# The z projection of a hybrid SSD encoder by groups of 512 columns in four PSUM banks, and a decay tile per direction

## The chip, the core and the metric

The kernel runs on one NeuronCore of a Trainium2 chip, on float32 data. The metric is the device time of one execution in microseconds (us). The engines are TensorE (PE: matmuls and transposes into PSUM banks), VectorE (DVE), ScalarE (ACT), GpSimd (POOL) and SyncE (SP, which issues the loads of weights).

## The reference

Two encoder layers over 512 tokens of width 1024. Each has a token-mixing sub-layer with one wide input projection, a pooling mixer and a bidirectional SSD mixer, and then a gated MLP with a depthwise convolution. What the change touches is the input projection's z part, the SSD mixer and its gated norm:

```python
proj = x @ w_in
u_pool, z, xbc, dt_raw, gate_logits = jnp.split(proj, list(IN_SPLITS), axis=-1)
xbc = jax.nn.silu(dwconv_centred(xbc, ssd_conv_w, ssd_conv_b))
xs, bm, cm = jnp.split(xbc, [SSD_INNER, SSD_INNER + gn], axis=-1)
y = bidirectional_ssd(xh, dt_raw, a_log, dt_bias, bm, cm, d_skip)
# per direction and head, by chunks of 128 tokens:
decay = jnp.exp(jnp.where(lower, a_cum[l] - a_cum[s], -jnp.inf))
y_diag = (C B^T * decay) x          # and a state carried from chunk to chunk
# gated norm, per group of 512 columns
v = y * jax.nn.silu(z)
v = v * lax.rsqrt(jnp.mean(v * v, axis=-1, keepdims=True) + RMS_EPS)
ssd_out = (v * g) @ w_ssd_proj
```

z and the SSD's inner width have 2048 columns: four groups of 512 columns, eight units of 256 columns (four heads of 64 each).

## The kernel before, in words

Every projection is made of three float32r matmuls per product (`mm3`, L297): each operand is cut into a high part and a remainder (`wh`, `wl` for weights, `xth`, `xtl` for x, transposed). `WeightStream` (L39) loads weight blocks of 1 MB through SP's queue into two buffers, and `_split` (L77) makes each half of a block into `wh` by a cast on ACT (L90) and `wl` by a subtraction on DVE (L91), three pairs of buffers. `get(ahead)` hands out the next pair and starts the splits `ahead` places on. The order of the blocks is written by `weight_plan` (L145).

Two PSUM pools have four banks each of 128x512 float32 (L252 to L260): `bank_a` for the projections, `bank_b` for small products and transposes. A bank goes to its next user when all readers of the last one are done.

PE's order is the order of the program text (`manual_schedule`, L280); the other engines get theirs from the scheduler, and each engine takes its instructions in its own fixed order. `Background` (L112) holds jobs, Python generators that emit a small piece of PE work and yield how many ticks their successor's data need. A tick, called between the matmuls of a projection, emits at most one piece, of the first job in the list that is ready.

For each layer and each group g of four (L1019): the columns B and C of the group (`bc`, two tiles of 128 features by 512 tokens), then unit 2g and unit 2g+1. `unit(u)` (L715) makes two x tiles (`xp`: 24 matmuls each, the weights stationary, 512 tokens moving), and gives each to `conv_silu` (L567): `conv` (L386) reads the bank by one ACT pass (L389) and four DVE taps (L395), and a Silu on ACT follows (L570). Then it makes the unit's z, token-major: for each of four chunks of 128 tokens, x's tile is stationary and 256 weight columns move, 8 x 3 matmuls per chunk, two chunks in one bank; a Silu (L736) takes each bank to `zs`.

Jobs run behind that: `bc_job` (transpose `btp`, scores `scp`), `x_job` (transpose `xt` to `xtok`), `unit_job` (L800: the weighted x `xw` on POOL, states `stp`, L835, their outputs `yop`, L862, then `zs` times `y`, L881, and per group `norm` with the squares `sq`, L891, and the transposes `ytp`), `heads_job` (L746) with `decay(h)` (L754) and the products `ydp` (L786). `decay` fetches the cumulative sums of both directions by one DMA on ACT's queue into a tile m of [128, 2, 512], masks each half on POOL (L761), takes eight exponentials of 128x128 on ACT (L768) and adds the halves on DVE (L769). Behind group 0 the dt job is finished, and behind group g > 0 the output projection `spp` of group g-1 runs (L922).

Of the kernel before, what the change touches and what calls it, by code (L numbers as in the profile page):

```python
# [9 lines left out]
F32 = mybir.dt.float32  # L10
# [7 lines left out]
P = 128  # L18
# [93 lines left out]
class Background:  # L112
    """Small pieces of TensorE work, put between the matmuls of the projections: one piece at
    most per tick; a piece says after how many ticks its successor's data can be there."""
# [5 lines left out]
    def spawn(self, gen, delay=0):  # L120
        job = Job(gen, self.now + delay)
        self.jobs.append(job)
        return job
# [21 lines left out]
def weight_plan(l, w_in, pool_w, w_ssd_proj, w_out, w_up, w_down):  # L145
# [37 lines left out]
    def unit(u):  # L183
        return pair(w_in, OFF_X + 256 * u) + ktiles(w_in, 0, KD, OFF_Z + 256 * u, 256)
# [37 lines left out]
def tile_hybrid_pool_ssd_convffn_encoder(  # L222
# [120 lines left out]
    def feature_tiles(name, n):  # L343
        """n column tiles [128 features, 512 tokens] of the next weights times x."""
# [12 lines left out]
    def first_tiles(name, n, fresh=False):  # L357
        """The same, by halves of the tokens, with what is left of x's transposes in between."""
# [27 lines left out]
    def conv(dst, ps, taps, bias):  # L386
        """Centred depthwise convolution along the tokens; taps are per-feature columns."""
# [12 lines left out]
    def rsqrt(pool, v, name):  # L400
        """v ** -0.5 of positive columns: a guess from the bits, then Newton's iteration."""
# [12 lines left out]
    def token_projection(l, name, src_h, src_l, kn, xcs, lnp, gt, bt, finish, final=False):  # L414
        """x <- LayerNorm(ALPHA * x + src @ w), token-major, by chunks of 128 tokens."""
# [9 lines left out]
        def root(c, mv):  # L425
            """(variance + EPS) ** -0.5, with a step of Newton's iteration."""
# [10 lines left out]
        def pieces(half, c):  # L437
            """The columns of a half that are summed and finished together."""
# [96 lines left out]
    for l in range(NL):  # L535
        # per-feature parameters as columns
# [46 lines left out]
        def make_bc(g, tiles):  # L583
# [4 lines left out]
            return bg.spawn(bc_job(g, bt, ct), 10)  # L588
# [126 lines left out]
        def unit(u):  # L715
# [3 lines left out]
            for i in range(2):  # L719
                (xps,) = feature_tiles(f"xp{nm}_{i}_", 1)  # L720
                cv = conv_silu(xps, 2 * u + i, f"xc{nm}_{i}")
                xjobs.append(bg.spawn(x_job(u, i, cv, xtok), 11))
            zs = sp.tile([P, NCH, 256], F32, tag="zs", name=f"zs{nm}", bufs=3)
            wz = [ws.get() for _ in range(2)]
            for cc in range(2):
                ps = bank_a(f"zp{nm}_{cc}")
                for ci in range(2):
                    c = 2 * cc + ci
                    s = slice(c * P, (c + 1) * P)
                    for k in range(KD):  # L730
                        wh, wl = wz[k // 4]
                        mm3(ps[:, ci * 256 : (ci + 1) * 256], xts["h"][:, k, s], xts["l"][:, k, s],
                            wh[:, k % 4, :], wl[:, k % 4, :], k == 0, k == KD - 1)
                        if k % 4 == 3:
                            bg.tick()
                nc.scalar.activation(  # L736
                    zs[:, 2 * cc : 2 * cc + 2, :],
                    ps.rearrange("p (c n) -> p c n", c=2), AF.Silu,
                )

            return bg.spawn(unit_job(u, xtok, zs, xjobs), 1)
# [4 lines left out]
        def heads_job():  # L746
            """The masked decay matrices of the heads, both directions, and the products with
            them within the chunks of 128 tokens."""
# [51 lines left out]
        def unit_job(u, xtok, zs, xjobs):  # L800
# [78 lines left out]
            while heads_done[0] < 4 * u + 4:  # L879
                yield 0  # L880
# [298 lines left out]
```

## Time and profile before

| what | value |
|---|---|
| median of 3 runs | 1991.07 us (1989.05 to 1992.81) |
| span of the profiled execution, first to last instruction | 1990.3 us |
| mean granted TensorE clock | 0.994 |
| PE busy | 1954.0 us, 98% |
| DVE busy | 1179.1 us, 59% |
| ACT busy | 947.9 us, 48% |
| POOL busy | 430.9 us, 22% |

The profiled execution has no time of its own beside its span; the span lies 0.8 us under the median of the runs. PE's rows overlap, because a matmul's row lasts until its modelled end; what a matmul costs in a stream is the step from one start to the next. The SSD stretch of layer 0, which the change rewrites, reaches from about 33 to 420 us, that of layer 1 from about 1020 to 1390 us.

### The profile page before, as it was taken

To read this page: it belongs to the slowest core of one execution; us is meant where nothing else is said; L and a number is where in the kernel's file an instruction comes from. 1 tells how busy PE (TensorE), PEld (TensorE's weight loads), DVE (VectorE), ACT (ScalarE), POOL (GpSimd) and SP (SyncE) were. 2 spreads that over 40 slices of the span, in tenths; PEclk is the share of its full clock that TensorE was granted. 3 is DMA by queue.
4 is the path that set the end of the run, shared out by engine and by line. 5 is a ranking of instruction groups with operands and counts; after the bars stand their busy time and mean duration, and the time that the engine had idled before them with its cause. 6 is when DMAs were issued, how large, how long until landed. Compare 5 with 4: busy or idle time off the path is not lost.

```text
span 1990.3 us, 27038 instructions
## 1 busy us (share of the span) xinstructions
PE 1954.0 (98%) x10614; PEld 1643.9 (83%) x10614; DVE 1179.1 (59%) x1796; ACT 947.9 (48%) x1629; POOL 430.9 (22%) x456
## 2 busy tenths in 40 slices
PE   8999999999999999999999999999999999999998
PEld 7878798988888888888888888989888888888886
DVE  5568576775556655543475685667656566555334
ACT  4767666644332544431257776656443334444321
POOL 1344424241111111110003344252411111111000
PEclk9999999999999999999999999999999999999999
DMA  5443424233241323232325434443333413322321
GB/s 159 127 116 116 127 92 141 85 112 114 79 162 51 106 94 110 94 128 92 97 93 154 115 112 118 116 120 104 90 111 91 169 43 106 106 85 92 129 89 72
DMA packets 172160, 214.87 MB, mean 108 GB/s; under 512 B 6752, under 2 KB 127748, under 8 KB 172032
## 3 DMA queue, kind: packets, MB, share of 16 engines
q1 hardware_dynamic: 151376, 170.14, 26.9%
q10 hardware_dynamic: 17712, 34.08, 6.5%
q0 software_dynamic: 2944, 8.91, 1.4%
q8 instruction: 84, 1.38, 0.3%
q14 instruction: 44, 0.36, 0.1%
HBM read 208.66 MB, written 4.46 MB: 107 GB/s over the span
## 4 chain that ended last, share of the span: by engine, by line
PE 86%; issue 7%; ACT 2%; DVE 2%; POOL 1%; DMA 1%; SPq 0%; ACTq 0%; POOLq 0%; DVEq 0%
PE fg L300 7%; PE fg L299 7%; PE fg L298 7%; PE dp L298 4%; PE dp L299 4%; PE dp L300 4%; PE spp L298 3%; PE spp L299 3%; PE spp L300 3%; PE zp L298 3%; PE zp L299 3%; PE zp L300 3%; PE xp L298 2%; PE xp L299 2%; PE xp L300 2%
## 5 line engine op out<-in xcount | busy, mean ns | idle before, releaser
L91 DVE TENSOR_TENSOR wl<-wraw,wh 128x1024 fp32r<-128x1024 f32 (+1 forms) x318 | 395.8, 1246 | 394.9 <-ACT wh L90 393.6
L90 ACT CAST wh<-wraw 128x1024 fp32r<-128x1024 f32 (+1 forms) x318 | 328.4, 1035 | 434.2 <-PE dp L300 121.9
L300 PE MATMUL fg<-xthm,wl 128*128 128x512 f32 x640 | 249.0, 389 | 0.0
L298 PE MATMUL fg<-xthm,wh 128*128 128x512 f32 x640 | 249.0, 389 | 0.0
L299 PE MATMUL fg<-xtlm,wh 128*128 128x512 f32 x640 | 249.0, 389 | 0.0
L768 ACT ACTIVATE m<-m,nac 128x128 f32<-128x128 f32 x512 | 158.5, 389 | 53.1 <-POOL m L761 52.8
L1122 POOL TENSOR_TENSOR cvv<-cvv,cg 128x512 f32<-128x512 f32 x44 | 56.6, 1286 | 412.8 <-DVE cvv L395 382.0
L299 PEld LDWEIGHTS fg<-xtlm,wh 128*128 128x128 f32 x640 | 120.2, 188 | 25.0
L298 PEld LDWEIGHTS fg<-xthm,wh 128*128 128x128 f32 x640 | 120.2, 188 | 24.9
L300 PEld LDWEIGHTS fg<-xthm,wl 128*128 128x128 f32 x640 | 120.2, 188 | 24.8
L298 PE MATMUL dp<-wh,ah 128*128 128x512 f32 (+1 forms) x352 | 136.6, 388 | 0.0
L300 PE MATMUL dp<-wh,al 128*128 128x512 f32 (+1 forms) x352 | 136.4, 387 | 0.0
L299 PE MATMUL dp<-wl,ah 128*128 128x512 f32 (+1 forms) x352 | 136.4, 387 | 0.0
L761 POOL TENSOR_SCALAR_AFFINE_SELECT m<-m 128x512 f32<-128x512 f32 x128 | 95.0, 767 | 179.6 <-DMA m<-acd 136.8
L298 PE MATMUL spp<-yth,wh 128*128 128x512 f32 x256 | 110.3, 431 | 0.5 <-ACT yth L916 0.5
L876 POOL TENSOR_TENSOR y<-y,yo 128x256 f32<-128x256 f32 x96 | 85.9, 904 | 103.0 <-DVE yo L868 100.2
L299 PE MATMUL spp<-ytl,wh 128*128 128x512 f32 x256 | 101.2, 395 | 0.7 <-DVE ytl L917 0.7
L300 PE MATMUL spp<-yth,wl 128*128 128x512 f32 x256 | 101.1, 395 | 0.0
L395 DVE SCALAR_TENSOR_TENSOR xc<-xp,pcwc,xc 128x510 f32<-128x510 f32 (+1 forms) x128 | 95.2, 745 | 7.7 <-ACT xc L389 6.1
L1125 ACT CAST ah<-cvv 128x512 fp32r<-128x512 f32 x44 | 27.3, 621 | 147.2 <-POOL cvv L1122 147.2
L512 POOL TENSOR_TENSOR x<-x,lnb 128x512 f32<-128x512 f32 x15 | 20.2, 1345 | 325.7 <-DVE x L508 316.1
L769 DVE TENSOR_TENSOR m<-m 128x512 f32<-128x512 f32 x64 | 45.8, 716 | 64.2 <-ACT m L768 54.9
(347 smaller groups left out, 4779.1 us busy)
## 6 DMA issues: line engine op xcount, KB each, us to landing
wraw<-in_w_in_dram SPq DMA_DIRECT2D x56, 1024.0 KB, 5.5
wraw<-in_w_up_dram SPq DMA_DIRECT2D x44, 1024.0 KB, 5.1
m<-acd ACTq DMA_DIRECT2D x64, 512.0 KB, 4.9
wraw<-in_w_down_dram SPq DMA_DIRECT2D x20, 1024.0 KB, 5.1
wraw<-in_w_ssd_proj_dram SPq DMA_DIRECT2D x16, 1024.0 KB, 5.1
wraw<-in_w_in_dram SPq DMA_DIRECT2D x16, 512.0 KB, 5.5
wraw<-in_w_out_dram SPq DMA_DIRECT2D x8, 1024.0 KB, 5.3
xi<-in_x_dram SPq DMA_DIRECT2D x4, 512.0 KB, 6.9
```

The source lines that it names most:

```text
L90: self.nc.scalar.copy(hv, src)
L91: self.nc.vector.tensor_tensor(lv, src, hv, op=ALU.subtract)
L298: nc.tensor.matmul(ps, lhsT=ah, rhs=bh, start=first, stop=False)
L299: nc.tensor.matmul(ps, lhsT=ah, rhs=bl, start=False, stop=False)
L300: nc.tensor.matmul(ps, lhsT=al, rhs=bh, start=False, stop=last)
L395: nc.vector.scalar_tensor_tensor(dst[:, o0:o1], ps[:, o0 + s : o1 + s], tap, dst[:, o0:o1], op0=ALU.mult, op1=ALU.add,)
L761: nc.gpsimd.affine_select(out=mv, in_=mv, pattern=[[0, NCH], [1 - 2 * d, P]], compare_op=ALU.is_ge, fill=NEG, base=0, channel_multiplier=2 ...
L768: nc.scalar.activation(mc, mc, AF.Exp, bias=nac[:, c, col : col + 1])
L769: nc.vector.tensor_tensor(m[:, 0], m[:, 0], m[:, 1], op=ALU.add)
L876: nc.gpsimd.tensor_tensor(y[:, c, :], y[:, c, :], yo[:, d, :], op=ALU.add)
L1122: nc.gpsimd.tensor_tensor(cv, cv, cg, op=ALU.mult)
L1125: nc.scalar.copy(h, cv)
```

## The change

`unit(u)` is taken apart. `x_unit(u)` makes the two x tiles and spawns the unit's job at once. `z_group(g)` runs once per group, between the two x units: z for 512 columns, four chunks of tokens in four banks. Its weight blocks are [512 rows of w_in, 512 columns], cut into four pairs of two 128-row tiles (two blocks and four pairs per group, as before). The first two pairs go through all four banks in turn, four products of 128 rows in each bank; with the last two pairs each chunk is finished and goes through its Silu. There are 16 ticks per group, as before. `bc_job` and `x_job` now go to the head of the list of jobs, and `bc_job` waits 7 ticks for 10. `decay` has a tile per direction, `m` (three buffers) and `mb` (two), each with a DMA of its own. `unit_job` waits for `zs_of[u]`. The pooling mixer sums in place, with its edge products taken first.

```diff
-    def unit(u):
-        return pair(w_in, OFF_X + 256 * u) + ktiles(w_in, 0, KD, OFF_Z + 256 * u, 256)
+    def xunit(u):
+        return pair(w_in, OFF_X + 256 * u)
+
+    def zgroup(g):
+        return [s for k in (0, 4) for s in ktiles(w_in, k, k + 4, OFF_Z + 512 * g, 512)]
...
-        seq += bc(g) + unit(2 * g) + unit(2 * g + 1)
+        seq += bc(g) + xunit(2 * g) + zgroup(g) + xunit(2 * g + 1)
...
-    def spawn(self, gen, delay=0):
+    def spawn(self, gen, delay=0, first=False):
         job = Job(gen, self.now + delay)
-        self.jobs.append(job)
+        self.jobs.insert(0 if first else len(self.jobs), job)
...
-            return bg.spawn(bc_job(g, bt, ct), 10)
+            return bg.spawn(bc_job(g, bt, ct), 7, True)
...
-                xjobs.append(bg.spawn(x_job(u, i, cv, xtok), 11))
-            zs = sp.tile([P, NCH, 256], F32, tag="zs", name=f"zs{nm}", bufs=3)
-            wz = [ws.get() for _ in range(2)]
-            for cc in range(2):
-                ps = bank_a(f"zp{nm}_{cc}")
...
+                xjobs.append(bg.spawn(x_job(u, i, cv, xtok), 11, True))
+            return bg.spawn(unit_job(u, xtok, xjobs), 1)
+
+        def z_group(g):
+
+            zg = sp.tile([P, NCH, 512], F32, tag="zs", name=f"zs{l}_{g}", bufs=2)
+            banks = [bank_a(f"zp{l}_{g}_{c}") for c in range(NCH)]
+
+            def product(c, k, wh, wl, kk):
+                s = slice(c * P, (c + 1) * P)
+                mm3(banks[c], xts["h"][:, k, s], xts["l"][:, k, s],
+                    wh[:, kk, :], wl[:, kk, :], k == 0, k == KD - 1)
+
+            for b in range(2):
+                wh, wl = ws.get()
+                for kk in range(2):
+                    for c in range(NCH):
+                        product(c, 2 * b + kk, wh, wl, kk)
+                        if c % 2:
                             bg.tick()
+            got = [ws.get(1) for _ in range(2)]
+            for c in range(NCH):
+                for b in range(2):
+                    wh, wl = got[b]
+                    for kk in range(2):
+                        product(c, 4 + 2 * b + kk, wh, wl, kk)
+                    bg.tick()
+                nc.scalar.activation(zg[:, c, :], banks[c], AF.Silu)
+            for i in range(2):
+                zs_of[2 * g + i] = zg[:, :, i * 256 : (i + 1) * 256]
...
-                m = sp.tile([P, 2, T], F32, tag="m", name=f"m{l}_{h}", bufs=3)
-                nc.scalar.dma_start(
-                    m, acd[l].rearrange("(d h) t -> d h t", d=2)[:, h, :].partition_broadcast(P)
-                )
-                for d in range(2):
-                    mv = m[:, d].rearrange("p (c t) -> p c t", c=NCH)
+                m = sp.tile([P, T], F32, tag="m", name=f"m{l}_{h}", bufs=3)
+                mb = sp.tile([P, T], F32, tag="mb", name=f"mb{l}_{h}", bufs=2)
+                for d, t in enumerate((m, mb)):
+                    col = d * 32 + h
+                    nc.scalar.dma_start(t, acd[l][col : col + 1, :].partition_broadcast(P))
...
-            while heads_done[0] < 4 * u + 4:
+            while heads_done[0] < 4 * u + 4 or u not in zs_of:
                 yield 0
+            zs = zs_of[u]
...
-            ujobs.append(unit(2 * g))
-            ujobs.append(unit(2 * g + 1))
+            ujobs.append(x_unit(2 * g))
+            z_group(g)
+            ujobs.append(x_unit(2 * g + 1))
```

The instructions move with it. PE's list has 9014 rows before and 8246 after, and ACT's list 85 table loads before and 125 after. In the rows below a line number is that of the file they come from, `xp_4_1` is the second x tile of unit 4, `zp_4_0` the first z bank of unit 4 (before), `zp_2_0` to `zp_2_3` the four z banks of group 2, whose units are 4 and 5 (after).

PE in layer 0 where z follows the x tiles of unit 4, before:

```order
L298 MATMUL xp_4_1_0_2620<-xthi,wh_2466 128x512
L299 MATMUL xp_4_1_0_2620<-xtli,wh_2466 128x512
L300 MATMUL xp_4_1_0_2620<-xthi,wl_2467 128x512
L298 MATMUL zp_4_0_2663<-wh_2536,xthi 128x256 [waits DVE_49,Activation_49]
L299 MATMUL zp_4_0_2663<-wl_2537,xthi 128x256 [waits DVE_49]
L300 MATMUL zp_4_0_2663<-wh_2536,xtli 128x256
```

PE at the same place after the change; `scp_2` is the score product of `bc_job`:

```order
L600 MATMUL scp_2_2452<-ct_2_2346,bt_2_2339 128x128 [waits DVE_49,Activation_49]
L600 MATMUL scp_2_2452<-ct_2_2346,bt_2_2339 128x128 x3
L301 MATMUL zp_2_0_2467<-wh_2356,xthi 128x512
L302 MATMUL zp_2_0_2467<-wl_2357,xthi 128x512
L303 MATMUL zp_2_0_2467<-wh_2356,xtli 128x512
L301 MATMUL zp_2_1_2468<-wh_2356,xthi 128x512
L302 MATMUL zp_2_1_2468<-wl_2357,xthi 128x512
L303 MATMUL zp_2_1_2468<-wh_2356,xtli 128x512
L301 MATMUL zp_2_2_2469<-wh_2356,xthi 128x512 [waits DVE_49]
L302 MATMUL zp_2_2_2469<-wl_2357,xthi 128x512
L303 MATMUL zp_2_2_2469<-wh_2356,xtli 128x512
L301 MATMUL zp_2_3_2470<-wh_2356,xthi 128x512 [waits DVE_49,Activation_49]
```

Before, z's first bank follows the x tile directly, and its rows wait for the weights. After, four banks are opened within twelve matmuls behind a `scp` piece, and the third and the fourth bank wait for DVE, the fourth for ACT as well.

DVE around the taps of that second x tile, before:

```order
L395 SCALAR_TENSOR_TENSOR xc_4_1_2645<-xp_4_1_0_2620,pcwc,xc_4_1_2645 128x510 [waits Activation_49]
L779 TENSOR_TENSOR m_16_2303<-m_16_2303,sct_2_2712 128x512 [waits Activation_49]
L395 SCALAR_TENSOR_TENSOR xc_4_1_2645<-xp_4_1_0_2620,pcwc,xc_4_1_2645 128x511 [waits DVE_49]
L779 TENSOR_TENSOR m_17_2363<-m_17_2363,sct_2_2712 128x512
L395 SCALAR_TENSOR_TENSOR xc_4_1_2645<-xp_4_1_0_2620,pcwc,xc_4_1_2645 128x511 [waits DVE_49]
L917 SCALAR_TENSOR_TENSOR ytl_1_2549<-ytp_1_0_2740,pcbc,yth_1_2548 128x512 [waits Activation_49]
L395 SCALAR_TENSOR_TENSOR xc_4_1_2645<-xp_4_1_0_2620,pcwc,xc_4_1_2645 128x510 [waits DVE_49]
L779 TENSOR_TENSOR m_18_2417<-m_18_2417,sct_2_2712 128x512
```

DVE around the same taps after the change (`m` decay tiles, `sct` the scores, `rs` the sum of the squares of the norm):

```order
L398 SCALAR_TENSOR_TENSOR xc_4_0_2399<-xp_4_0_0_2360,pcwc,xc_4_0_2399 128x510 [waits DVE_49]
L91 TENSOR_TENSOR wl_2474<-wraw_2471,wh_2473 128x1024 [waits DMAHW0_49,PE_49,Activation_49]
L793 TENSOR_TENSOR m_16_2187<-m_16_2187,sct_2_2457 128x512 [waits Activation_49]
L793 TENSOR_TENSOR m_17_2249<-m_17_2249,sct_2_2457 128x512
L398 SCALAR_TENSOR_TENSOR xc_4_1_2459<-xp_4_1_0_2410,pcwc,xc_4_1_2459 128x510 [waits PE_49,Activation_49]
L793 TENSOR_TENSOR m_18_2308<-m_18_2308,sct_2_2457 128x512
L398 SCALAR_TENSOR_TENSOR xc_4_1_2459<-xp_4_1_0_2410,pcwc,xc_4_1_2459 128x511 [waits DVE_49] x2
L910 TENSOR_TENSOR rs_1_2503<-ss_1_2486 128x4 [waits Activation_49]
L398 SCALAR_TENSOR_TENSOR xc_4_1_2459<-xp_4_1_0_2410,pcwc,xc_4_1_2459 128x510 [waits DVE_49]
```

The four taps stand in both behind and between products with the scores; now a weight remainder and two products stand ahead of the first tap, and the norm's sum ahead of the last.

ACT ahead of its pass over that x tile, after the change:

```order
L590 ACT_TABLE_LOAD [waits DVE_49]
L590 ACTIVATE ct_2_2346<-ct_2_2346 128x512 [waits Activation_49]
L782 ACT_TABLE_LOAD [waits DMAHW3_49]
L782 ACTIVATE mb_20_2728<-mb_20_2728,nac_672 128x128 [waits Pool_49]
L595 COPY btok_2_2439<-btp_2_2440 128x512 [waits PE_49]
L90 CAST wh_2473<-wraw_2471 128x1024 [waits DMAHW0_49,PE_49]
L906 ACTIVATE sq_1_0_0_2487,ss_1_2486<-zs_1_1191 128x256 [waits Pool_49]
L573 ACT_TABLE_LOAD [waits DVE_49]
L573 ACTIVATE xc_4_0_2399<-xc_4_0_2399 128x512 [waits Activation_49]
L602 COPY sct_2_2457<-scp_2_2452 128x512 [waits PE_49]
L392 ACTIVATE xc_4_1_2459<-xp_4_1_0_2410,pcbc,pcwc 128x512
```

And before:

```order
L389 ACTIVATE xc_4_0_2609<-xp_4_0_0_2540,pcbc,pcwc 128x512 [waits PE_49]
L90 CAST wh_2655<-wraw_2653 128x1024 [waits DMAHW6_49,PE_49]
L570 ACTIVATE xc_4_0_2609<-xc_4_0_2609 128x512 [waits DVE_49,Activation_49]
L592 COPY btok_2_2688<-btp_2_2689 128x512 [waits PE_49]
L389 ACTIVATE xc_4_1_2645<-xp_4_1_0_2620,pcbc,pcwc 128x512 [waits PE_49]
L599 COPY sct_2_2712<-scp_2_2707 128x512
```

The pass over the second x tile (`xc_4_1<-xp_4_1`) now has the three table loads, the square and the score copy ahead of it; before, the copy of the scores came behind it.

## Rows read from the trace of the kernel before

**Rows 1.** the page's span and busy time: us, share, instructions.
```profile
span 1990.3 us, 27038 instructions
...
PE 1954.0 (98%) x10614; PEld 1643.9 (83%) x10614; DVE 1179.1 (59%) x1796; ACT 947.9 (48%) x1629; POOL 430.9 (22%) x456
```

**Rows 2.** waits of PE: us in total, times, longest.
```profile
PE stp L835 <- POOL xw L818: 6.5, 4, 2.1
```

**Rows 3.** timeline of PE, z of unit 7, 24 starts: start, us.
```profile
384.31 0.28 PE L298 MATMUL zp<-wh,xthi 128*128 128x256 f32 x1
...
387.06 0.28 PE L300 MATMUL zp<-wh,xtli 128*128 128x256 f32 x1
```

**Rows 4.** timeline of PE, output projection, first and last of 57 starts.
```profile
604.74 0.40 PE L299 MATMUL op<-wl,mh 128*128 128x512 f32 x1
...
617.60 0.39 PE L298 MATMUL op<-wh,mh 128*128 128x512 f32 x1
```

**Rows 5.** timeline of unit 5: last x matmul, last tap of its convolution.
```profile
284.81 0.40 PE L300 MATMUL xp<-xthi,wl 128*128 128x512 f32 x1
...
289.92 0.74 DVE L395 SCALAR_TENSOR_TENSOR xc<-xp,pcwc,xc 128x510 f32<-128x510 f32 x1
```

**Rows 6.** timeline of unit 0, engines PE and DVE: the same two places.
```profile
44.41 0.39 PE L300 MATMUL xp<-xthi,wl 128*128 128x512 f32 x1
...
54.33 0.74 DVE L395 SCALAR_TENSOR_TENSOR xc<-xp,pcwc,xc 128x510 f32<-128x510 f32 x1
```

**Rows 7.** chain of waits, PE's pieces between the matmuls: start, us.
```profile
408.76 0.44 PE xt L576 x4
...
413.82 0.86 PE yop L862 x4
```

**Rows 8.** groups by form, ACT and DVE: busy us, mean ns of one.
```profile
L90 ACT CAST wh<-wraw 128x1024 fp32r<-128x1024 f32 x308 | 322.3, 1048 | 416.1 <-PE dp L300 117.3 <-PE spp L299 62.4 <-PE g1p L299 40.6
...
L768 ACT ACTIVATE m<-m,nac 128x128 f32<-128x128 f32 x512 | 158.5, 389 | 53.1 <-POOL m L761 52.8
...
L768 ACT ACT_TABLE_LOAD x30 | 38.5, 1283 | 15.6 <-DMA m<-acd 15.3
...
L891 ACT ACTIVATE sq<-zs 128x256 f32<-128x256 f32 x64 | 25.7, 404 | 2.0 <-POOL y L876 2.0
...
L389 ACT ACTIVATE xc<-xp,pcbc,pcwc 128x512 f32<-128x512 f32 x32 | 24.7, 771 | 4.5 <-PE scp L597 4.5
...
L570 ACT ACTIVATE xc<-xc 128x512 f32<-128x512 f32 x32 | 20.1, 629 | 24.5 <-DVE xc L395 24.2 <-DVE rsi L411 0.2
...
L599 ACT COPY sct<-scp 128x512 f32<-128x512 f32 x8 | 4.7, 584 | 0.0
...
L91 DVE TENSOR_TENSOR wl<-wraw,wh 128x1024 fp32r<-128x1024 f32 x308 | 388.6, 1263 | 383.6 <-ACT wh L90 382.6
...
L779 DVE TENSOR_TENSOR m<-m,sct 128x512 f32<-128x512 f32 x64 | 49.1, 770 | 0.8
...
L395 DVE SCALAR_TENSOR_TENSOR xc<-xp,pcwc,xc 128x511 f32<-128x511 f32 x64 | 47.7, 746 | 1.1
...
L868 DVE TENSOR_TENSOR yo<-yop,ef 128x512 f32<-128x512 f32 x32 | 22.0, 686 | 19.1 <-PE yop L862 18.8
```

**Rows 9.** busy us of PE, PEld, DVE, ACT, POOL, then clock; timeline of PE.
```profile
120.00:125.00 5.00, 1.70 (x9) 1.07 (x8) 4.60 (x5) 1.21 (x3) 3.72 (x3) 1.00 0.21 68
...
125.00:128.40 3.40, 3.40 (x18) 3.06 (x18) 1.08 (x2) 2.01 (x3) 3.40 (x4) 0.50 0.00 0
...
126.10 0.41 PE L298 MATMUL zp<-wh,xthi 128*128 128x256 f32 x1
...
127.81 0.41 PE L300 MATMUL zp<-wh,xtli 128*128 128x256 f32 x1
```

**Rows 10.** one issue on the ACT queue; busy us as in rows 9.
```profile
117.95 0.37 ACTq L756 DMA_DIRECT2D m<-acd  x1
...
100.00:200.00 100.00, 94.12 (x629) 79.65 (x627) 76.72 (x124) 71.47 (x154) 41.40 (x42) 0.98 0.40 114
```

More of the change, by code (lines that the diff above doesn't have):

```diff
@@ L713, in x_job, with x_unit @@
             yield 1
-        def unit(u):
+        zs_of = {}
+        def x_unit(u):
             nm = f"{l}_{u}"
@@ L721, in unit @@
                 cv = conv_silu(xps, 2 * u + i, f"xc{nm}_{i}")
-                xjobs.append(bg.spawn(x_job(u, i, cv, xtok), 11))
-            zs = sp.tile([P, NCH, 256], F32, tag="zs", name=f"zs{nm}", bufs=3)
-            wz = [ws.get() for _ in range(2)]
-            for cc in range(2):
-                ps = bank_a(f"zp{nm}_{cc}")
[L727 to L734, printed above, removed]
-                            bg.tick()
-                nc.scalar.activation(
-                    zs[:, 2 * cc : 2 * cc + 2, :],
-                    ps.rearrange("p (c n) -> p c n", c=2), AF.Silu,
-                )
-            return bg.spawn(unit_job(u, xtok, zs, xjobs), 1)
+                xjobs.append(bg.spawn(x_job(u, i, cv, xtok), 11, True))
[13 more added lines that the diff above has]
+                        if c % 2:
+                            bg.tick()
+            got = [ws.get(1) for _ in range(2)]
[8 more added lines that the diff above has]
+                zs_of[2 * g + i] = zg[:, :, i * 256 : (i + 1) * 256]
         ytiles = {}
@@ L754, in decay @@
             def decay(h):
-                m = sp.tile([P, 2, T], F32, tag="m", name=f"m{l}_{h}", bufs=3)
-                nc.scalar.dma_start(
-                    m, acd[l].rearrange("(d h) t -> d h t", d=2)[:, h, :].partition_broadcast(P)
-                )
-                for d in range(2):
-                    mv = m[:, d].rearrange("p (c t) -> p c t", c=NCH)
+                m = sp.tile([P, T], F32, tag="m", name=f"m{l}_{h}", bufs=3)
[3 more added lines that the diff above has]
+                    nc.scalar.dma_start(t, acd[l][col : col + 1, :].partition_broadcast(P))
+                    mv = t.rearrange("p (c t) -> p c t", c=NCH)
                     nc.gpsimd.affine_select(
@@ L765, in decay @@
                     for c in range(NCH):
-                        mc = m[:, d, c * P : (c + 1) * P]
-                        col = d * 32 + h
+                        mc = t[:, c * P : (c + 1) * P]
                         nc.scalar.activation(mc, mc, AF.Exp, bias=nac[:, c, col : col + 1])
-                nc.vector.tensor_tensor(m[:, 0], m[:, 0], m[:, 1], op=ALU.add)
+                nc.vector.tensor_tensor(m, m, mb, op=ALU.add)
                 ms[h] = (m, bg.now)
@@ L778, in heads_job @@
                     yield 0
-                nc.vector.tensor_tensor(m[:, 0], m[:, 0], grp[u // 2][2], op=ALU.mult)
+                nc.vector.tensor_tensor(m, m, grp[u // 2][2], op=ALU.mult)
                 yield 2
@@ L787, in heads_job @@
                             ps[q * 64 : (q + 1) * 64, c * 64 : (c + 1) * 64],
-                            lhsT=m[:, 0, t0 : t0 + 64],
+                            lhsT=m[:, t0 : t0 + 64],
                             rhs=xtok[:, c, hh * 64 : (hh + 1) * 64], start=True, stop=True,
@@ L798, in heads_job, with unit_job @@
                 yield 1
-        def unit_job(u, xtok, zs, xjobs):
+        def unit_job(u, xtok, xjobs):
             nm = f"{l}_{u}"
@@ L965, in pooling @@
                     src, span = s, span * 2
-                win = s[:, 8 - half : 8 - half + T]
-                pd = pp.tile([P, T], F32, tag="pd", name=f"pd{nm}", bufs=1)
+                win = pd = s[:, 8 - half : 8 - half + T]
+                ends = pp.tile([P, 2, 8], F32, tag="ends", name=f"ends{nm}", bufs=1)
                 uc = u[:, 8 : T + 8]
+                for e, t0 in ((0, 0), (1, T - half)):
+                    nc.vector.tensor_tensor(
+                        ends[:, e, :half], win[:, t0 : t0 + half], edge[:, g, e, :half],
+                        op=ALU.mult,
+                    )
                 nc.vector.scalar_tensor_tensor(
@@ L973, in pooling @@
                     nc.vector.tensor_tensor(
-                        pd[:, t0 : t0 + half], win[:, t0 : t0 + half], edge[:, g, e, :half],
-                        op=ALU.mult,
-                    )
-                    nc.vector.tensor_tensor(
-                        pd[:, t0 : t0 + half], pd[:, t0 : t0 + half], uc[:, t0 : t0 + half],
+                        pd[:, t0 : t0 + half], ends[:, e, :half], uc[:, t0 : t0 + half],
                         op=ALU.subtract,
```

## The prediction

> **What bounds the kernel now.** I read the page's table of busy time first. TensorE (PE) is busy in 1954.0 of 1990.3 us [rows 1], so a change pays only if it shortens PE's own stream or one of its few waits. The list of PE's waits comes next: the longest that belongs to the stretch changed here is `stp` on GpSimd's `xw`, 6.5 us in four waits, two per layer [rows 2]. Then the timelines give the step from one matmul to the next, which is the price of a matmul in a stream (the 0.28 or 0.39 us of a row overlap). In the z projection 24 matmuls of 256 columns start from 384.31 to 387.06 us: 2.75 / 23 = 0.1196 us each [rows 3]. A stream of the form that z gets, with x's tile stationary and 512 weight columns moving, is the output projection: 57 starts from 604.74 to 617.60 us, 12.86 / 56 = 0.2296 us each [rows 4].
>
> **Half as many, wider z matmuls.** Per layer z goes from 768 matmuls of 256 columns to 384 of 512 (PE's list shrinks from 9014 to 8246 rows, 768 over both layers). Before: 1536 x 0.1196 = 183.7 us. After: 768 x 0.2296 = 176.3 us. PE gains **7.4 us**. Background ticks stay at 16 per group, so the pieces between cost what they cost. In rows, one matmul costs some 13 to 16 ns over its columns at 2.4 GHz (0.1196 less 0.1067, 0.2296 less 0.2133), and the halving saves part of that. The Trainium skill, page "TensorE: Matmul & The Clock Gate", section "Back-to-back issue gap", puts this fixed part at 2.5 ns: by it z would go from 167.7 to 165.7 us, an estimate from that page, the gain would be only 2 us and the sum 5 us higher. The measured steps decide, and they are the ones used in the sum.
>
> **The new wait: four banks at once.** The pool that serves z has four banks. Before, a unit's z took one bank at a time, and the two banks that its x projection had just filled could be emptied at leisure. Now z opens all four in its first 12 matmuls, so its third and fourth are the banks of the two x tiles just made. The fourth is free only when the second x tile has been convolved: one ScalarE (ACT) pass and four VectorE (DVE) taps. PE's list shows the wait in front of `zp_2_3`, and everything behind it on PE waits too. It is due after one step, one `scp` piece of 0.44 us (as the four-transpose piece in [rows 7]) and nine steps: 0.23 + 0.44 + 2.07 = 2.7 us after the last x matmul starts. The shortest convolution in the trace of before, of all 32 x tiles, has its last tap end at 290.66 us, 5.85 us after that start at 284.81 us [rows 5]. So each group stalls by 5.85 - 2.7 = 3.1 us at the least, 8 x 3.1 = **25 us** over eight groups.
>
> What it is likely to be needs a walk through the queues, since ACT and DVE take their rows in the order listed.
> - Group 0: the order of DVE up to this convolution is nearly that of before, with the steps of the dt series between its taps; there it ended at 55.07 us after a last x matmul at 44.41 us [rows 6]. With both bc pieces now ahead of z, the fourth bank is due at 44.41 + 0.23 + 0.88 + 2.07 = 47.6 us. Stall 7.5 us.
> - Group 2, with 0 at the start of the last x matmul and durations from [rows 7, 8]. PE finishes `yop_3_1` at -8.8 us (30 steps and four pieces earlier). Behind it DVE does yo 0.69, two taps of ct 1.5, a weight remainder 1.26 and ct's last tap 0.75, and is there at some -4.3. Then ACT: table load 1.28, Silu 0.63, table load 1.28, exponential 0.39, copy 0.58, weight cast 1.05, square 0.40, table load 1.28, Silu 0.63, copy of sct 0.58 (3.8 us), and only then the pass over the x tile, done at 4.6. DVE has two products m x sct to do when sct is there (5.35), then tap, product, two taps, a sum that needs the squares, and the last tap: 9.4. Due at 2.7, so a stall of 6.7 us.
> - Group 1: ACT, after Silu of ct at -0.9, has a table load, eight exponentials (with a wait of 0.75 for their row), a cast, a table load, a Silu and two copies ahead, and finishes the pass at 8.5; four taps (3.1) end at 11.6. A `yop` piece moves the due time to 3.1. Stall 8.5 us. Group 3: ACT's pass ends at 5.5, DVE's last tap with a product between at 10.0, due 3.1: 6.9 us.
>
> Sum per layer 7.5 + 8.5 + 6.7 + 6.9 = 29.6 us, and layer 1 has the same program: **59 us**. Nothing covers it, as PE has no other work released.
>
> **The clock.** In 120 to 125 us PE was busy in only 1.70 us, and in the next 3.4 us the granted clock was 0.50 (1.2 GHz), with z's steps at 0.214 us instead of 0.120 [rows 9]. A stall of 7 us leaves as long a hole. I price half of 3.4 us, 1.7 us, for each: 8 x 1.7 = **13.6 us** (lower bound nothing, upper bound the whole 3.4 us, 27 us).
>
> **What goes away.** The two waits for `xw` lie in group 1 just behind z's start; the x job now starts earlier and PE comes later, so I take all 6.5 us back and the half-clock stretch that follows them, 2 x 1.7 us: **9.9 us**.
>
> **The other edits.** A decay tile per direction makes 64 issues on ACT's queue into 128, at 0.37 us of its sequencer each [rows 10]: 24 us, mostly beside ACT's own work. ACT's list has 125 table loads for 85; 40 x 1.283 us [rows 8] = 51 us more on an engine that is 71% busy in 100 to 200 us [rows 10]. What lies on the path is in the walks above; the rest I set at nothing, covered by ACT's idle time, and if that cover is gone it is the fourth case below. The bc pieces moved ahead find their Silu done in the walks (group 1 within 0.2 us). Exponentials, masks and products are as many as before. Pooling's edge steps are the same five operations in another order, off PE's path: nothing. Weight blocks are as many and as large, with rows of 2 KB for 1 KB, and never waited for by PE: nothing.
>
> **Sum.** Against the profiled execution's span: 1990.3 - 7.4 + 59 + 13.6 - 9.9 = 2045.6 us. The median of the runs, 1991.07 us, lies 0.8 us above that span, so I say **2046 us**.
>
> **The rivals.**
> - *The convolution comes through at once.* The walks may be too slow where a row is ready early. At the 3.1 us of [rows 5] the time is 1991 - 17.3 + 25 = 1999 us, with the clock falling 2012 us. For it: that span is measured. Against: it was an idle moment of ACT, and 40 table loads come on top. Chance 0.2.
> - *Faster.* The z gain and the `xw` waits together are 17.3 us. They win if the bank comes free within 2.7 + 17.3 / 8 = 4.9 us of the last x matmul, clock included; wholly hidden, the time is 1974 us. For it: PE is never shown waiting for z's banks now. Against: none of 32 convolutions made 5.85 us. Chance 0.06.
> - *ACT becomes the bound of the stretch.* Its 75 us of new table loads and issues then fall on the path in half, in front of the decay products and state pieces: 2046 + 38 = 2084 us. For it: 71% busy, in-order queues. Against: each stall of PE lets ACT catch up. Chance 0.2.
> - That z isn't halved can't be: PE's list shows it.
>
> **How the numbers follow.** Forecast 0.54 (2015 to 2070 us). 80% range: 1999 to 2086 us, from the first rival's least to the third's price; above and below it I leave 0.2. A measurement of this kernel tells about 0.2%, 4 us, from no change. Faster than that needs the second rival: 0.06. Within 0.2%, between it and the first: 0.04. Slower: 0.90.
>
> **What would show it.** In the changed kernel's profile, z's steps should be 0.23 us; PE's waits should be led by `zp` on DVE's `xc` tap, eight of some 7 us, one per group in front of the fourth bank; PE's busy time should be less by some 50 us than the span; the granted clock should be 0.5 behind each. The forecast is wrong if these waits are under 3 us, or if larger waits of PE stand at `stp`, `ydp` or `btp`.

## The result and the profile after

The changed kernel takes 2084.14 us in the median of 4 runs (2081.43 to 2085.66), the kernel before 1991.94 us beside it (1989.05 to 1996.57, 4 runs): a ratio of 1.0461, with a 95% interval of 1.0445 to 1.0478. It is slower by 92 us where 55 were forecast.

The page of the changed kernel, as in [rows 1]:

```profile
span 2082.6 us, 25692 instructions
...
PE 1973.1 (95%) x9846; PEld 1616.0 (78%) x9846; DVE 1186.1 (57%) x1796; ACT 1009.9 (48%) x1669; POOL 418.9 (20%) x456
```

The span grew by 92.3 us. PE's time without work (span less busy time) grew from 36.3 to 109.5 us, by 73.2; its busy time grew by 19.1 us although it has 768 matmuls less. So two things are to be found: who made PE wait, and why its work took longer.

PE's waits after the change, which answer to [rows 2] (us in total, times, longest):

```profile
PE zp L301 <- DVE xc L398: 37.5, 8, 6.1
PE btp L579 <- ACT bt L573: 14.2, 4, 6.3
PE zp L301 <- DVE rs L911: 12.8, 2, 6.4
PE spp L302 <- DVE ytl L932: 8.8, 8, 2.3
PE spp L301 <- ACT yth L931: 8.2, 6, 2.9
...
PE xt L579 <- ACT xc L573: 4.9, 2, 2.4
```

z's banks lead: 37.5 + 12.8 = 50.3 us. The two waits put down to `rs`, the small row behind the tap in DVE's list, stand in front of a fourth bank too: group 2 waits first at its third bank, for 1.17 us from 287.0, and then at its fourth.

```profile
295.53 0.76 PE L301 MATMUL zp<-wh,xthi 128*128 128x512 f32 x1 [6.42 <-DVE rs L911]
```

The waits for `xw` are gone. But 14.2 us stand at `btp`, 17.0 at `spp` (1.2 before) and 4.9 at `xt`: 34.9 us more at places that the forecast had at nothing.

The stall of group 0, which answers to [rows 6]: PE's timeline, then ACT's and DVE's (start, us, engine, line, instruction, [idle before it <- what ended that]).

```profile
49.50 0.39 PE L303 MATMUL zp<-wh,xtli 128*128 128x512 f32 x1
55.86 0.77 PE L301 MATMUL zp<-wh,xthi 128*128 128x512 f32 x1 [5.97 <-DVE xc L398]
```

```profile
51.31 0.78 ACT L392 ACTIVATE xc<-xp,pcbc,pcwc 128x512 f32<-128x512 f32 x1
```

```profile
54.97 0.74 DVE L398 SCALAR_TENSOR_TENSOR xc<-xp,pcwc,xc 128x510 f32<-128x510 f32 x1
```

The first row is z's ninth matmul, the next opens the fourth bank. ACT makes its pass over the second x tile at 51.31 us, the last tap ends at 54.97 + 0.74 = 55.71 us, and PE goes on 0.15 us later. PE was there at 49.50 + 0.23 = 49.73 us, so the mechanism is the forecast one, with 6.0 us for 7.5.

z's step, answering to [rows 3, 4]: 11 starts in PE's timeline of group 1.

```profile
166.66 0.40 PE L302 MATMUL zp<-wl,xthi 128*128 128x512 f32 x1
...
168.97 0.40 PE L303 MATMUL zp<-wh,xtli 128*128 128x512 f32 x1
```

2.31 / 10 = 0.231 us, for 0.2296 forecast.

The clock, answering to [rows 9] (stretch, length, busy us of PE, PEld, DVE, ACT, POOL, then granted clock):

```profile
49.50:54.50 5.00, 0.39 (x2) 0.00 (x0) 4.75 (x10) 2.58 (x4) 0.00 (x0) 1.00 0.01 2
54.50:61.30 6.80, 5.44 (x13) 4.31 (x14) 4.59 (x12) 2.33 (x3) 0.54 (x1) 0.50 0.04 3
143.24:150.06 6.82, 4.43 (x11) 3.50 (x12) 2.17 (x3) 5.58 (x8) 2.38 (x3) 0.50 0.00 0
290.01:300.25 10.24, 4.72 (x11) 3.79 (x12) 8.82 (x28) 9.59 (x24) 0.00 (x0) 0.50 0.00 0
399.24:406.06 6.82, 3.55 (x8) 2.82 (x9) 3.48 (x6) 3.48 (x9) 0.47 (x1) 0.50 0.00 0
109.10:112.52 3.42, 3.21 (x10) 2.58 (x10) 1.17 (x2) 3.36 (x5) 0.69 (x2) 0.50 0.77 281
129.58:136.41 6.83, 3.34 (x10) 2.85 (x11) 6.42 (x10) 5.21 (x9) 2.23 (x4) 0.50 0.20 40
```

Around each z stall the clock stays at 0.50 (1.2 GHz) for 6.8 or 10.2 us, where 3.4 were taken from before. Over the whole run the mean granted clock is 0.975 for 0.994, which is 0.025 x 2082.6 - 0.006 x 1990.3 = 40 us of full rate lost. PE was busy in 24.7 of the 40.9 us of the six half-rate rows, 60%, so about 24 us of it fell on work; with z's 7.4 us off, that is 17 of the 19.1 us by which PE's busy time grew. All half-rate stretches of the two traces give the same: PE was busy in them for 65.2 us after and 16.6 before, and half of the difference, 24.3 us, is what its work lost. Of that 17.6 us stand at z's eight stalls and 10.0 at other waits (`btp`, `xt` and `spp` among them, less what other waits cost before), and 3.3 us are gone with the stretches behind the waits for `xw`.

The new wait at `btp` in group 1, PE, ACT and DVE:

```profile
126.38 0.40 PE L303 MATMUL xp<-xthi,wl 128*128 128x512 f32 x1
133.07 1.11 PE L579 MATMUL btp<-ident,bt 128*128 128x128 f32 x4 [6.30 <-ACT bt L573]
```

```profile
128.16 0.76 ACT L392 ACTIVATE xc<-xp,pcbc,pcwc 128x512 f32<-128x512 f32 x1
131.09 1.28 ACT L573 ACT_TABLE_LOAD   x1 [2.18 <-DVE bt L398]
132.39 0.63 ACT L573 ACTIVATE bt<-bt 128x512 f32<-128x512 f32 x1
```

```profile
128.34 2.02 DVE L783 TENSOR_TENSOR m<-m,mb 128x512 f32<-128x512 f32 x1 [0.35 <-issue]
130.28 0.74 DVE L398 SCALAR_TENSOR_TENSOR bt<-bc,pcwc,bt 128x510 f32<-128x510 f32 x1
```

bt's last tap stands behind a sum of decay tiles, bt's Silu behind that tap and a table load, and PE, for whom `bc_job` is now the first job and due after 7 ticks, stands still from 126.61 us on, while the next x tile's 24 matmuls stand behind `btp` in its list. The sum itself starts 0.1 us after the exponentials that it needs (the last two end at 128.25 us), and takes 2.02 us, where the mean of the 64 such sums is 0.79; no run shows why.

### The profile page after: what moved, and what is told of

It reads as the page before. It is cut to its first block, busy times and chain, and to the rows that moved or that the text cites. A ratio compares the mean times of both kernels' runs of the same rounds, so it can differ in the third digit from the quotient of the medians.

```text
span 2082.6 us, 25692 instructions
## 1 busy us (share of the span) xinstructions
PE 1973.1 (95%) x9846; PEld 1616.0 (78%) x9846; DVE 1186.1 (57%) x1796; ACT 1009.9 (48%) x1669; POOL 418.9 (20%) x456
## 3 DMA queue, kind: packets, MB, share of 16 engines
q8 instruction: 78, 1.28, 0.3%
## 4 chain that ended last, share of the span: by engine, by line
PE 76%; issue 6%; DVE 6%; ACT 5%; DMA 4%; POOL 2%; ACTq 0%; POOLq 0%; SPq 0%; DVEq 0%
PE fg L303 7%; PE fg L302 7%; PE fg L301 7%; PE dp L301 4%; PE dp L302 4%; PE dp L303 4%; PE zp L301 3%; PE zp L303 3%; PE zp L302 3%; PE spp L302 3%; DMA m<-acd 3%; PE spp L303 3%; PE spp L301 3%; DVE xc L398 2%; PE xp L301 2%
## 5 line engine op out<-in xcount | busy, mean ns | idle before, releaser
L782 ACT ACTIVATE m<-m,nac 128x128 f32<-128x128 f32 x256 | 82.8, 392 | 57.7 <-POOL m L776 57.1
L890 POOL TENSOR_TENSOR y<-y,yo 128x256 f32<-128x256 f32 x96 | 79.3, 832 | 136.9 <-DVE yo L882 133.9
L776 POOL TENSOR_SCALAR_AFFINE_SELECT m<-m 128x512 f32<-128x512 f32 x64 | 47.9, 748 | 220.2 <-DMA m<-acd 172.5
L782 ACT ACTIVATE mb<-mb,nac 128x128 f32<-128x128 f32 x256 | 84.6, 393 | 9.3 <-POOL mb L776 8.0
L783 DVE TENSOR_TENSOR m<-m,mb 128x512 f32<-128x512 f32 x64 | 50.6, 791 | 62.8 <-ACT m L782 49.2
```

The costliest lines, as they stand in the source:

```text
L776: nc.gpsimd.affine_select(out=mv, in_=mv, pattern=[[0, NCH], [1 - 2 * d, P]], compare_op=ALU.is_ge, fill=NEG, base=0, channel_multiplier=2 ...
L782: nc.scalar.activation(mc, mc, AF.Exp, bias=nac[:, c, col : col + 1])
L783: nc.vector.tensor_tensor(m, m, mb, op=ALU.add)
L890: nc.gpsimd.tensor_tensor(y[:, c, :], y[:, c, :], yo[:, d, :], op=ALU.add)
```

## The experiments

Two theories at first. **Bank theory**: the loss is z's four banks opened at once, and what PE waits for there. **ACT theory**: ACT has 40 table loads and 64 issues more, its queue is late everywhere, and a wait that is removed turns up at the next piece. After the first four runs a **job-order theory** (the `bc` pieces are asked for too early) and after the next four a **rhythm theory** (x of one unit, bc and x of the next group now follow each other with no z between) came in. Each text set off below was written before its run. All times are medians; every ratio is to the kernel before on the same chip.

| kernel | us | ratio (95%) | PE idle, us | clock |
|---|---|---|---|---|
| before | 1991.9 | 1 | 36.3 | 0.994 |
| changed | 2084.1 | 1.0461 (1.0445 to 1.0478) | 109.5 | 0.975 |
| before, decay tile per direction | 1999.0 | 1.0036 (1.0026 to 1.0047) | 40.8 | 0.992 |
| changed, old decay tile | 2117.1 | 1.0639 (1.0618 to 1.0660) | 126.6 | 0.967 |
| changed, five banks | 2042.3 | 1.0248 (1.0233 to 1.0263) | 77.2 | 0.984 |
| changed, z chunk first | 2036.2 | 1.0220 (1.0204 to 1.0236) | 74.5 | 0.987 |
| chunk first, five banks | 2043.1 | 1.0261 (1.0244 to 1.0278) | 75.2 | 0.983 |
| changed, narrow z | 2042.4 | 1.0258 (1.0240 to 1.0275) | 72.7 | 0.989 |
| five banks, bc at 10 ticks | 2051.9 | 1.0307 (1.0292 to 1.0323) | 84.3 | 0.985 |
| chunk first, bc at 10 ticks | 2056.3 | 1.0322 (1.0304 to 1.0339) | 85.9 | 0.982 |
| chunk first, five banks, bc at 10 | 2047.3 | 1.0279 (1.0264 to 1.0295) | 75.2 | 0.983 |
| before, stages in the new order | 2055.4 | 1.0323 (1.0308 to 1.0339) | 83.6 | 0.982 |
| changed, z in two halves | 2067.2 | 1.0379 (1.0361 to 1.0396) | 96.7 | 0.977 |
| z in two halves, old job order | 2038.3 | 1.0235 (1.0219 to 1.0250) | 73.4 | 0.986 |

PE idle is the profiled span less PE's busy time. No kernel beat the one before.

**The decay tile per direction, alone in the kernel before.** `decay` as in the change, nothing else.

> The kernel before with one edit of the change: a decay tile per direction with a DMA each; z, the order of the jobs and the pooling mixer as before. ACT's list has 103 table loads for 85. Bank theory (the loss comes from z opening four banks at once): no wait of PE for z, 1985 to 1998 us. ACT theory (the loss comes from table loads and issues that the two decay tiles put on ACT): at least a third of the 92 us, 2022 us or more, with waits of PE at ydp or stp.

It costs 7 us, with 18 table loads more (ACT has 1647 instructions for 1629) and all 64 added issues. A row of PE's waits that was not among those of before:

```profile
PE xt L576 <- ACT xc L570: 6.2, 2, 3.1
```

It is the largest new wait; in all PE's idle time grew by 4.5 us and its busy time by 2.8. The time lies 1 us above the bank theory's range, and far below the ACT theory's 2022 us and the 38 us of the forecast's third rival.

**The old decay tile in the changed kernel.** `decay` put back to one tile of [128, 2, 512] and one DMA; for room one of the two `g1` tiles of the gate shares a buffer with the pooling mixer's `us`.

> The changed kernel with one decay tile and one DMA for both directions, as before (two gate tiles of the later gates share a buffer of the pooling mixer to make room). ACT's list has 97 table loads for 125. Bank theory: the waits of zp stay over 35 us and the time is 2060 to 2085 us. ACT theory: the waits of zp fall under 20 us and the time is 2035 us or less.

Neither time came: it is 33 us slower than the changed kernel, though z's waits (29.7 us put down to `xc`, 7.4 to `rsi`) are over 35 us as the bank theory had them, and ACT has only 12 table loads more than before (1641 instructions for 1629). Waits of PE:

```profile
PE spp L301 <- ACT yth L932: 24.9, 8, 4.8
PE btp L579 <- ACT bt L573: 19.0, 5, 9.2
PE scp L600 <- ACT ct L590: 13.2, 2, 7.1
```

So the number of table loads doesn't rank these kernels, and that part of the ACT theory falls; its other part, that a wait taken away turns up at the next piece, comes back below. The extra waits are at `spp`, `btp` and `scp`, not in the pooling stage alone (`pop` has 6.9 us); what the shared `g1` buffer adds wasn't separated, so the 33 us aren't shown to be the decay tile's.

**Three ways to take z's bank wait away.** A fifth bank for the projections, with three left for the small products:

```diff
-name="psa", bufs=4
+name="psa", bufs=5
-name="psb", bufs=4
+name="psb", bufs=3
```

> The changed kernel with five banks for the projections and three for the small products, for four and four. z's fourth bank is then that of the first x tile, convolved some 7 us earlier. Bank theory: the 50 us of waits of zp fall under 15, the half clock behind them goes, and the time is 2015 to 2045 us; btp and spp still wait. ACT theory: the waits move to other places and the time stays over 2070 us.

z's first weights taken chunk by chunk, so that a bank is opened every 12 matmuls:

```diff
-            for b in range(2):
-                wh, wl = ws.get()
-                for kk in range(2):
-                    for c in range(NCH):
+            got = [ws.get(1) for _ in range(2)]
+            for c in range(NCH):
+                for b in range(2):
+                    wh, wl = got[b]
+                    for kk in range(2):
                         product(c, 2 * b + kk, wh, wl, kk)
...
```

> The changed kernel with z's first two weight pairs held together and used chunk by chunk, 12 matmuls in one bank before the next is opened. The fourth bank is then due 36 steps of 0.23 us, 8.3 us, after z's start for 2.1. Bank theory: the waits of zp fall from 50 us to under 10 and the time is 2005 to 2035 us; a short new wait for the fourth weight pair is possible. ACT theory: over 2070 us.

And z put back to units of 256 columns and a bank at a time, both units where `z_group` stands, all else as changed:

> The changed kernel with z alone put back to 256 columns, one unit after the other in the same place (bc, x of unit 2g, z of both units, x of unit 2g+1), a bank at a time; decay tiles, jobs at the head of the list and pooling as in the changed kernel. Bank theory: z's 50 us of waits and some 25 us of the half-rate stretches behind them go, 7.4 us of narrower matmuls come back: 2000 to 2030 us. Rhythm theory: the six tiles in a row stay and ACT and DVE are as late, PE waits for other pieces in place of z's banks: 2045 to 2090 us, with its waits still 60 us or more in sum.

They gain 42, 48 and 42 us on the changed kernel: five banks within the bank theory's range, chunk first 1 us above it. PE's waits, five banks first, then chunk first, then narrow z:

```profile
PE btp L579 <- ACT bt L573: 15.5, 2, 7.7
...
PE zp L301 <- DVE xc L398: 0.9, 2, 0.5
```

```profile
PE btp L579 <- ACT bt L573: 18.5, 4, 10.6
PE spp L301 <- ACT yth L931: 11.0, 6, 2.9
```

```profile
PE btp L579 <- ACT bt L573: 15.3, 4, 7.1
PE spp L301 <- ACT yth L924: 13.8, 6, 4.6
```

Three different edits, one result: the four banks are worth 42 to 48 of the 92 us, and some 44 to 50 us remain with z's banks out of the way. The bank theory holds for about half of the loss. Narrow z fell between what the two theories expected of it (2030 and 2045 us).

Chunk first and a fifth bank together:

> Chunk-first z and a fifth bank for the projections together. Bank theory: z's waits, 7.0 us with the chunk-first order alone and 0.9 us with the fifth bank alone, are under 1 us, and the btp waits stay at 15 to 20 us: 2022 to 2034 us. ACT theory: the 7 us turn up at another piece, 2034 to 2046 us.

```profile
PE btp L579 <- ACT bt L573: 9.8, 2, 4.9
PE ytp L926 <- DVE ytl L932: 8.3, 4, 2.6
```

z's waits for taps are gone, btp's 18.5 us have become 9.8, and still it is 7 us slower than chunk first alone. PE waits at `ytp` now until the last `ytp` bank has been read by `ytl`: the small pieces have three banks for four. The time is in the ACT theory's range and 9 us above the bank theory's.

**bc's pieces asked for three ticks later.** `bc_job(g, bt, ct), 7, True` becomes `10, True`, in chunk first, in chunk first with five banks, and in five banks.

> The chunk-first z of the earlier run (2036.2 us, where PE waits 18.5 us at btp for the Silu of bt and 7.0 us at z's banks), with bc_job at 10 ticks in place of 7, still at the head of the list. Job-order theory: what is left there is mostly that seven ticks ask for bt's transposes before its Silu is done; three ticks more are about 4.1 us (three times six steps of 0.23 us), so btp's four waits fall from 18.5 to under 6 us, a half-clock stretch goes with them, time 2005 to 2024 us. ACT theory: ACT's queue is late by its 40 further table loads, so whatever comes next waits instead (scp, xt, ydp or z's banks), time 2028 to 2045 us.

> Chunk-first z, a fifth bank and bc_job at 10 ticks. Bank and job-order theories together: neither zp nor btp waits by more than 6 us in all, what stays is spp's waits (about 15 us in the chunk-first run) and their clock: 1993 to 2015 us. ACT theory: 2025 us or more, with the waits at other pieces and their sum still over 45 us.

> A fifth bank and bc_job at 10 ticks, z's first half through all four banks as in the changed kernel. Bank and job-order theories: from 2042.3 us (fifth bank alone) btp's 15.5 us and the half-clock stretches behind them (6.8 us each) go, 2012 to 2030 us. ACT theory: the waits move to ytp, spp and ydp, 2034 to 2046 us.

All three miss the job-order theory: they are 20, 4 (the intervals overlap) and 10 us slower than the same kernels with 7 ticks. The second is where the ACT theory had it, the first and the third lie above its ranges too. In the first and the third `btp` is gone from PE's waits as expected (in the second 10.0 us stay there), but chunk first with 10 ticks has

```profile
PE spp L301 <- ACT yth L931: 13.9, 6, 3.8
PE zp L301 <- DVE xc L398: 12.4, 6, 5.4
PE zp L301 <- ACT m L782: 11.5, 2, 5.8
```

and five banks with 10 ticks has

```profile
PE zp L301 <- DVE xc L398: 19.0, 6, 5.0
```

PE now comes to z's banks before the taps of bt and x are through. So a wait of PE at `btp` seems to have been time for DVE and ACT as well; that is a reading of these rows, not a run. The old job order with the four-bank z wasn't tried. By the program's order z's later banks would then wait for taps that stand on DVE behind work on scores that PE makes only after z, and the kernel would stop; this is argued, not shown.

**The order of the stages alone, in the kernel before.** z stays 256 wide and a bank at a time; old decay tile, old pooling, and the jobs in their old order. A unit's job is now spawned behind its x tiles, as in the change, and waits for its z.

```diff
-        seq += bc(g) + unit(2 * g) + unit(2 * g + 1)
+        seq += bc(g) + xunit(2 * g) + zunit(2 * g) + zunit(2 * g + 1) + xunit(2 * g + 1)
...
-            ujobs.append(unit(2 * g))
-            ujobs.append(unit(2 * g + 1))
+            ujobs.append(x_unit(2 * g))
+            z_unit(2 * g)
+            z_unit(2 * g + 1)
+            ujobs.append(x_unit(2 * g + 1))
```

> The kernel before, with nothing changed but the order within a group: bc, x of unit 2g, z of both units, x of unit 2g+1, with z still 256 columns wide and a bank at a time, the old decay tile and the old jobs. Rhythm theory: x of one unit, bc of the next group and x of its first unit, six tiles with a convolution each, now stand in a row with no z between them; in such a row of the changed kernel DVE was busy in 18.4 and ACT in 17.9 of 23.7 us, both fall behind there and PE waits for whatever it needs next, without any wide z: 2010 to 2045 us, with PE's waits 25 us or more above those of before. Bank theory: no z bank of 512 columns is opened behind an x tile, so nothing is lost: 1985 to 2000 us.

64 us slower, above both ranges: this reordering costs that much with no wide z, no new decay tile and no new order of the list of jobs. PE's idle time grew by 47 us. Its waits:

```profile
PE up L301 <- DVE rsi L414: 17.9, 2, 9.0
PE ydp L794 <- issue: 15.6, 2, 7.8
PE spp L301 <- ACT yth L925: 9.2, 6, 4.0
```

The largest is a place of its own: `up` is the pooling projection, which now comes right behind the second x unit of group 1, and its first matmul waits 9 us per layer while that unit's taps and the steps of the norm (`rsi`) take turns on DVE. The changed kernel has no wait at `up`, so the 64 us can't be read as this move's share of the 92.

The `ydp` wait of group 1 in layer 0 is one that the profile names no cause for ("issue"). PE's timeline around it, then ACT's:

```profile
114.70 0.60 PE L579 MATMUL xt<-ident,xc 128*128 128x128 f32 x4
...
128.71 1.12 PE L794 MATMUL ydp<-xtok,m 128*64 128x64 f32 x16 [7.79 <-issue]
```

```profile
111.02 1.05 ACT L90 CAST wh<-wraw 128x1024 fp32r<-128x1024 f32 x1 [6.64 <-PE xp L302]
111.97 4.79 ACT L776 ACTIVATE m<-m,nac 128x128 f32<-128x128 f32 x16
...
122.68 1.28 ACT L573 ACT_TABLE_LOAD   x1
123.98 0.63 ACT L573 ACTIVATE bt<-bt 128x512 f32<-128x512 f32 x1
124.61 1.28 ACT L776 ACT_TABLE_LOAD   x1
...
128.04 1.05 ACT L713 COPY xtok<-xt 128x512 f32<-128x512 f32 x2
```

`ydp` takes `xtok`, and starts 0.1 us after the first of these two copies can have ended. PE had made its transposes by 115.30 us; the copy came 12.7 us later, at the end of an unbroken run of ACT: two casts, 24 exponentials, four table loads, two Silu and two passes. ACT had sat idle for 6.64 us in front of that run, behind a weight cast that waited for PE's x tile, with the exponentials in line behind it. So at this place ACT is what the ACT theory says, the bound, first by waiting in order and then with 4 x 1.28 = 5.1 us of table loads; this kernel has 20 more of them than before (1649 instructions for 1629).

The reason in the expectation, that a row of six tiles overloads ACT and DVE, isn't borne out. In 28 us of x and bc tiles just ahead, PE, PEld, DVE, ACT and POOL are busy for

```profile
71.00:99.00 28.00, 28.00 (x163) 22.58 (x163) 21.16 (x27) 22.47 (x46) 13.36 (x12) 1.00 0.55 161
```

76% for DVE and 80% for ACT, and PE doesn't wait at all; over the whole row of six tiles, 71 to 118 us, it is 71% and 74%. What changed is which work stands ahead of the piece that PE asks for next.

**z in two halves, x and z in turn again.** z stays 512 wide; chunks 0 and 1 in two banks behind x of unit 2g, chunks 2 and 3 behind x of unit 2g+1, with z's weights loaded and cut twice.

```diff
-            ujobs.append(x_unit(2 * g))
-            z_group(g)
-            ujobs.append(x_unit(2 * g + 1))
+            for i in range(2):
+                ujobs.append(x_unit(2 * g + i))
+                z_half(g, i)
```

> The changed kernel with z, still 512 columns wide, in two halves of two chunks and two banks each, the first behind x of unit 2g, the second behind x of unit 2g+1; the weights of a group's z are loaded and cut twice for that (32 pairs more in all, about 34 us of ACT and 40 us of DVE at 1.05 and 1.26 us each). Decay tiles, jobs and pooling as in the changed kernel. Rhythm theory: two z banks stand behind each pair of x tiles as before, the waits go, 1978 to 2000 us. Bank theory: z's own waits go, btp's 14 us and the others stay, 2005 to 2030 us. ACT theory: ACT and DVE get still more work, 2030 us or more.

And the same with `bc_job` and `x_job` at the end of the list, `bc_job` at 10 ticks, as before:

> The same half-z kernel with bc_job and x_job at the end of the list and bc_job at 10 ticks, as before the change. Job-order theory: over 8 us below the half-z run, as PE asks for bt later. Rhythm theory: within 8 us of it, 1978 to 2000 us, as neither order makes PE wait once x and z alternate.

The rhythm theory missed both, and the bank theory the first; the ACT theory's 2030 us or more was met there, and the job-order theory's 8 us in the second. With the new job order PE waits at `xt`, with the old one hardly there:

```profile
PE xt L579 <- ACT xc L573: 28.0, 4, 8.3
```

```profile
PE pop L301 <- ACT ph L992: 8.6, 2, 4.3
PE xp L301 <- ACT zs L746: 8.6, 2, 4.3
```

The old job order is worth 29 us here, 2067 to 2038. The edit moves `bc_job` and `x_job` together; by the waits it is the `x_job` at the head of the list that makes PE stand before `xt` while later pieces could go. So the job order is a third loss, shown by itself. It leaves 47 us with x and z in turn, among them 8.6 us that this form of half brings itself (both of its banks end together, and the next x tile waits for their Silu) and 32 pairs of weights more.

## Why the prediction was right, and where its size was off

The sign, the place and the mechanism of the largest term held; the sum was 37 us short. The measured 2084 us lies above the forecast's own 2015 to 2070 us, and 2 us inside the 80% range only because that range reached up to the third rival's price, for ACT's work in front of the decay products and state pieces. The changed kernel has no wait of PE at `ydp` or `stp`, so that it fell inside is luck. Of the signs named beforehand, z's step, the eight waits at the fourth banks (5.6 to 6.4 us for some 7) and the clock of 0.5 at them came as said; the span exceeds PE's busy time by 109.5 us, where some 50 were named, and the two waits at `btp` are each as long as one of z's (6.3 us), though the sum at `btp` is smaller.

| step | forecast, us | measured, us |
|---|---|---|
| wider z matmuls | -7.4 | step 0.231 for 0.2296 |
| z's banks | +59 | +50.3 |
| half clock at z's stalls | +13.6 | +17.6 |
| half clock at other waits | 0 | +10.0 |
| waits for `xw` | -6.5 | -6.5 |
| half clock behind them | -3.4 | -3.3 |
| other waits of PE | 0 | +29.4 |

The measured column adds to 90 us with z's 7.4 taken as forecast; the 2 us to 92.3 are left without a cause. So the 37 us that the sum lacks are the other waits and their clock, 39.4 us, and the 2 left over, less 4.7 by which z's stalls and their clock came out lower than forecast. The last row is PE's growth in idle time, 73.2, less 50.3, plus 6.5.

- *Wider z matmuls.* Right by its step. The Trainium skill, page "TensorE: Matmul & The Clock Gate", section "Back-to-back issue gap", gives, by its formula for a single matmul's gap with 2.5 ns over the columns, a step of 0.216 us, an estimate from that page; the trace shows 0.231 and decides.
- *z's banks.* Right in kind and within a fifth in size: ten waits, eight at fourth banks and two short ones at the third of group 2, and the largest term of the result. Where z opens a bank at a time again, or has a bank more, 42 to 48 us come back.
- *The clock.* Mis-sized. "I price half of 3.4 us, 1.7 us, for each": the half-rate stretches at z's stalls are 6.8 and 10.2 us, but the stall itself fills part of them, and PE's work in them lost 1.5 to 2.7 us each, 17.6 us in sum. That is inside the step's bounds. The larger miss is the 10.0 us at other waits, for which the sum has no term.
- *"The bc pieces moved ahead find their Silu done in the walks (group 1 within 0.2 us)."* This failed. Group 1 waits 6.30 us, twice. The walk of that group names ACT's rows alone up to the pass over the x tile; bt's last tap stood on DVE behind a decay sum that itself waits for ACT's exponentials.
- *What was not costed at all* is the move of the second x unit from between two z stages to the place in front of the next group's bc. The sum has no term for it. Alone it costs 64 us in the kernel before, in part at a place (`up`) where the changed kernel doesn't wait. In the changed kernel 44 to 50 us remain when z's banks are out of the way; this move, the new places of the jobs, the decay tile and the pooling edit are all in them.
- *The decay tile.* "The rest I set at nothing": 7 us alone, so nearly right; in the changed kernel it may be a gain, since 33 us are added without it and with the shared `g1` buffer. That the third rival's 2084 us is the time measured is chance: its price was 75 us of ACT's work on the path in half, and the kernel with the four-bank z and the fewest table loads is the slowest of all.

What stays open: how much of the remaining half goes to the stage order and how much to the jobs and the other edits, since the single losses (64 us, 29 us, 42 to 48 us) don't add up; why the kernel with the old decay tile beside the wide z is slower; and the pooling edit, which no run took alone. A new order of stages also makes the scheduler put ACT's and DVE's rows in another order, and no run held those fixed.

## What to carry to other kernels

Before a stage is widened so that it opens all banks of its pool at once, count from the row of the last user's release, not from its matmuls: here eight stalls of some 6 us ate a gain of 7.4 us nearly seven times over. Where PE's order is fixed, and stages are moved past each other, cost the move by itself: walk ACT's and DVE's lists together for every piece that PE will ask for, because a tap behind a sum behind an exponential is one chain, and a cast that waits for a weight buffer holds up every exponential behind it. And a wait that is taken away may be the time in which the other engines catch up: in seven kernels in which z's waits or btp's were taken down, PE's idle time stayed between 72 and 86 us.

## What the runs showed of the hardware that was not expected

The half-rate stretches are not of one length: 3.4 us after a wait of 2.4 us at `xt` (109.10 to 112.52 us), 6.8 us with waits of 5.6 to 6.3 us, 10.2 us where a stall of 6.4 us followed one of 1.2 us. They begin before the engine is back at work: at `zp` of group 0 the clock fell at 54.5 us and PE started at 55.86. What the work lost didn't grow with the length of the stretch in the same way, since the longer ones cover more of the stall: PE was busy for 3.2 us of the 3.4 at `xt`, for 3.3 of the 6.8 at `btp`, and for 3.0 to 5.5 of the 6.8 or 10.2 at z's stalls. At half rate that is 1.6, 1.7 and 1.5 to 2.7 us lost; in sum the half rate took about 24 us from PE's work beside 73 us of added waits.
